# A four-layer decoder trunk: GpSimd makes the norm's diagonals and the recurrence's constants, and ScalarE's table functions keep program order

## The chip, the cores and the metric

One core of a Trainium2 chip runs the kernel in one launch. The metric is device time in microseconds (us), the median of several runs. In the profile, PE is TensorE's matmul, PEld its weight load, DVE is VectorE, ACT is ScalarE, POOL is GpSimd and SP is SyncE, whose queue issues the DMAs.

## The reference

The input is 256 tokens of width 1024 in float32. Four layers follow each other; each is a token mixer and a squared-ReLU MLP (1024 to 4096 to 1024), both behind an RMS norm and added to the residual. The mixers are a gated linear recurrence (layers 0 and 3), a chunked spatial gating unit (layer 1) and a short gated convolution (layer 2). A last RMS norm ends it. What matters here is the norm and the recurrence mixer:

```python
def _rmsnorm(x, g):
    x32 = x.astype(jnp.float32)
    y = x32 * lax.rsqrt(jnp.mean(x32 * x32, axis=-1, keepdims=True) + EPS)
    return y.astype(x.dtype) * g

def _rglru_mixer(h, w_in, conv_w, conv_b, gate_a_w, gate_a_b, gate_x_w, gate_x_b, lam, w_out):
    gate, xr = jnp.split(h @ w_in, 2, axis=-1)          # D_RNN = 1280 each
    gate = jax.nn.gelu(gate)
    xr = _causal_dwconv(xr, conv_w) + conv_b
    xh = xr.reshape(b, s, A_HEADS, A_HEAD_DIM)
    r = jax.nn.sigmoid(jnp.einsum("bshi,hij->bshj", xh, gate_a_w).reshape(b, s, D_RNN) + gate_a_b)
    ig = jax.nn.sigmoid(jnp.einsum("bshi,hij->bshj", xh, gate_x_w).reshape(b, s, D_RNN) + gate_x_b)
    log_a = -LRU_C * r.astype(jnp.float32) * jax.nn.softplus(-lam.astype(jnp.float32))
    a = jnp.exp(log_a)
    u = jnp.sqrt(-jnp.expm1(2.0 * log_a)) * (ig * xr).astype(jnp.float32)
    _, hs = lax.associative_scan(_lru_combine, (a, u), axis=1)   # h = a * h_before + u
    return (hs.astype(h.dtype) * gate) @ w_out

def _sqrelu_mlp(h, w1, w2):
    return jnp.square(jax.nn.relu(h @ w1)) @ w2
```

## The kernel before

**Layout.** Features lie on the 128 partitions and the 256 tokens along the free dimension. Eight feature tiles make up the residual. Intermediates are kept in pairs of two tiles (128 x 512).

**Products.** Each float32 product is made of three TensorE matmuls of a rounded format: the weight is split into a high and a low part, the activation too, and high by high, high by low and low by high are added up (`mm3`, L164). Weights come in chunks of up to 2048 columns by DMA from SP's queue into `raw`; ACT casts each 1024 columns to the high part (`whi`, L135), DVE subtracts to get the low part (`wlo`, L136). These two steps are called the cast and the split of the weights below. Up to five chunks are held at a time, so a new cast can begin when PE has finished with an old chunk. The gates' block-diagonal weights and the spatial weights are used whole, in plain float32 (L451, L578).

**The norm.** The gain is multiplied into the activations at once (`prep`, L195 and L196), and the token's scale 1/rms is applied after the product, when the result is read from PSUM. `Scales.first` sums the squares over the features with a small matmul (L245), then makes the reciprocal root without a table: ACT copies the sum (L228), and POOL does a seed and three Newton steps, 13 operations of 128x2 (L229 to L235), and splits the result into a high and a low part (L251, L252). Four multiplies of the 128x128 unit matrix by a column of these (L257, on DVE) make diagonal matrices `diag`. `Scales.second` multiplies them by ones on PE (L263), which lays the scales along the free dimension in every partition, and ACT copies that row to SBUF (L267, `rs`). `first` and `second` are called from hooks within the running product, in most places five of the eight steps of a 512-column product apart. The last norm of all uses the square root's table and DVE instead (`table=True`).

**The recurrence mixer** goes through `LRU_ORDER`: three branch products with the short convolution behind them (L417 to L436), a first gate product with GELU (`gated`, L489, L490), the two gates of the first five tiles (`gates(0)`, L451 and tanh at L455), the recurrence of pairs 0 and 1 (`recur`), the gates of the other five tiles, the recurrence of pairs 2 to 4, and the rest of the gate products. `recur` makes the decay by tanh and exp (L467) with per-channel constants `lam2` and `lam4`, takes a square root (L475), ends the coefficient with an affine step on DVE (L478) and runs the scan (L481). `meet` multiplies state and gate (L498) and splits the result (L329 on ACT, L330 on DVE) for the output product. `softplus_lambda` makes the constants at the start from a series in s = t / (t + 2), on DVE (L386 to L401, each 128x20).

**Order.** PE's instructions keep the order in which they are written. Those of the other engines are put in order ahead of time by a scheduler, by priority and by a model of when each is ready; every engine then runs its own queue strictly in that order. `recur` and the second half of `Scales.first` have raised priority, the weights' loads, casts and splits lowered.

Of the kernel before, what the change touches and what calls it, by code (L numbers as in the profile page):

```python
# [9 lines left out]
F32 = mybir.dt.float32  # L10
F32R = mybir.dt.float32r
I32 = mybir.dt.int32
AF = mybir.ActivationFunctionType
# [16 lines left out]
LRU_C = 8.0  # L30
# [41 lines left out]
def trunk(ctx: ExitStack, tc: tile.TileContext, xT, consts, sbias, weights, out, widths, whole, causal):  # L72
    nc = tc.nc
    MULT, ADD, SUB, MAX = ALU.mult, ALU.add, ALU.subtract, ALU.max
# [24 lines left out]
    def wtile(dtype=F32, name="wk"):  # L99
        return wide.tile([P, 2, T], dtype, name=name, tag="wk", bufs=N_WIDE)  # L100

    def bank():
        return psum.tile([P, 512], F32, name="ps", tag="ps")
# [39 lines left out]
    def next_chunk():  # L143
        i = used[0]
        used[0] += 1
        while asked[0] < n_chunks:
            ahead = sum(n not in whole for n in range(i + 1, asked[0]))
            if asked[0] > i and ahead + (asked[0] not in whole) > AHEAD:
                break
            with tc.high_priority(offset=-LATER):  # L150
                for load, part in fetch(asked[0]):
                    load()
                    part()
            asked[0] += 1
        return ready.pop(i)
# [17 lines left out]
    eye = const.tile([P, P], F32, name="eye")  # L173
# [64 lines left out]
    class Scales:  # L238
# [3 lines left out]
        def first(self, table=False):  # L242
            ps = bank()
            for c in range(2):
                nc.tensor.matmul(ps[:, 2 * c:2 * c + 2], sq_now[0][:, c * P:(c + 1) * P], ones[:, :2],  # L245
                                 start=True, stop=True)
            with tc.high_priority(offset=SOON):
                self.col = rsqrt(ps[:, 0:4].rearrange("p (c two) -> p c two", two=2)[:, :, 0], table)
                eng = nc.vector if table else nc.gpsimd
                hi, lo = (work.tile([P, 2], F32R, name="rc2", tag="rc2", bufs=4) for _ in range(2))  # L250
                eng.tensor_copy(out=hi, in_=self.col)  # L251
                eng.tensor_tensor(out=lo, in0=self.col, in1=hi.bitcast(F32), op=SUB)  # L252
                self.diag = []
                for part in (hi, lo):
                    diag = work.tile([P, 2, P], F32R, name="diag", tag="diag", bufs=4)
                    for c in range(2):
                        nc.vector.tensor_scalar_mul(diag[:, c, :], eye, part.bitcast(F32)[:, c:c + 1])  # L257
                    self.diag.append(diag.rearrange("p c t -> p (c t)"))

        def second(self, copy=True):  # L260
# [8 lines left out]
    def both(r):  # L269
        return r.unsqueeze(1).broadcast_to([P, 2, T])  # L270
# [102 lines left out]
    lam2 = const.tile([P, 2 * KR], F32, name="lam2")  # L373
    lam4 = const.tile([P, 2 * KR], F32, name="lam4")
    half_b = const.tile([P, 4 * KR], F32, name="half_b")

    def softplus_lambda():

        n = 2 * KR

        def small():
            return work.tile([P, n], F32, name="sp", tag="sp", bufs=8)

        lam = cst[:, CONST_AT["a_lam"]:CONST_AT["a_lam"] + n]
        neg, mag, t, d, s, s2, q = (small() for _ in range(7))
        nc.vector.tensor_scalar_mul(neg, lam, -1.0)  # L386
        nc.vector.tensor_tensor(out=mag, in0=lam, in1=neg, op=MAX)
        nc.scalar.activation(t, mag, AF.Exp, scale=-1.0)
        nc.vector.tensor_scalar_add(d, t, 2.0)
        nc.vector.reciprocal(out=d, in_=d)  # L390
        nc.vector.tensor_tensor(out=s, in0=t, in1=d, op=MULT)
        nc.vector.tensor_tensor(out=s2, in0=s, in1=s, op=MULT)
        nc.vector.tensor_scalar_mul(q, s2, 1.0 / 19.0)
        for i in range(17, 1, -2):
            nc.vector.scalar_tensor_tensor(out=q, in0=q, scalar=1.0 / i, in1=s2, op0=ADD, op1=MULT)
        nc.vector.scalar_tensor_tensor(out=q, in0=q, scalar=1.0, in1=s, op0=ADD, op1=MULT)
        nc.vector.tensor_scalar_max(neg, neg, 0.0)
        nc.vector.scalar_tensor_tensor(out=q, in0=q, scalar=2.0, in1=neg, op0=MULT, op1=ADD)
        nc.vector.tensor_scalar_mul(lam2, q, LRU_C / 4)
        nc.vector.tensor_scalar_mul(lam4, q, -LRU_C / 2)  # L400
        nc.vector.tensor_scalar_mul(half_b, cst[:, CONST_AT["a_ba"]:CONST_AT["a_ba"] + 4 * KR], 0.5)  # L401

    def mixer_a(layer):
        scale = Scales()
        xc = []
        beside = {}
        for g in range(KR // GRP):
            pairs = [wtile(name="be") for _ in range(2)]
            beside.update({(g, m + 1): pairs[m // 2][:, m % 2, :] for m in range(GRP - 2)})
        rg, ig = ([wtile(name=n) for _ in range(KR // 2)] for n in ("rg", "ig"))  # L410
# [28 lines left out]
        def gates(g):  # L439

            own = [xc[(g * GRP + m) // 2][:, (g * GRP + m) % 2, :] for m in range(GRP)]
            near = [own[1]] + [beside[g, m] for m in range(1, GRP - 1)] + [own[GRP - 2]]
            at = 0
            for m in range(GRP):
                mt = g * GRP + m
                ps = bank().rearrange("p (j t) -> p j t", t=T)
                for e in range(2):
                    for n, x in enumerate((own[m], near[m])):
                        if at % 8 == 0:
                            w = next_chunk().rearrange("p (k w) -> p k w", w=P)  # L450
                        nc.tensor.matmul(ps[:, e, :], w[:, at % 8, :], x, start=n == 0, stop=n == 1)  # L451
                        at += 1
                for e, dst in enumerate((rg, ig)):
                    c = (2 * e + layer) * KR + mt
                    nc.scalar.activation(dst[mt // 2][:, mt % 2, :], ps[:, e, :], AF.Tanh, scale=0.5,  # L455
                                         bias=half_b[:, c:c + 1])

        def recur(pairs):


            th, qs = {}, {}
            for i in pairs:
                th[i], qs[i] = wtile(name="th"), wtile(name="q")
                for dst, fn, lam in ((th[i], AF.Tanh, lam2), (qs[i], AF.Exp, lam4)):
                    for j in range(2):
                        c = layer * KR + 2 * i + j
                        nc.scalar.activation(dst[:, j, :], rg[i][:, j, :], fn, scale=lam[:, c:c + 1],  # L467
                                             bias=lam[:, c:c + 1])
                nc.vector.tensor_scalar_add(qs[i], qs[i], 1.0)
                t = rg[i]  # L470
                nc.vector.scalar_tensor_tensor(out=t, in0=th[i], scalar=1.0, in1=qs[i], op0=ADD, op1=MULT)
                nc.vector.scalar_tensor_tensor(out=qs[i], in0=t, scalar=4.0, in1=qs[i], op0=SUB, op1=MULT)
                nc.vector.scalar_tensor_tensor(out=ig[i], in0=ig[i], scalar=1.0, in1=xc[i], op0=ADD, op1=MULT)
            for i in pairs:
                nc.scalar.activation(th[i], th[i], AF.Sqrt)  # L475
                nc.vector.scalar_tensor_tensor(out=th[i], in0=qs[i], scalar=-0.25, in1=th[i], op0=MULT, op1=MULT)
                nc.vector.tensor_tensor(out=ig[i], in0=ig[i], in1=th[i], op=MULT)  # L477
                nc.vector.tensor_scalar(out=qs[i], in0=qs[i], scalar1=-0.5, scalar2=-1.0, op0=MULT, op1=ADD)  # L478
                h = xc[i]
                for j in range(2):  # L480
                    nc.vector.tensor_tensor_scan(out=h[:, j, :], data0=qs[i][:, j, :], data1=ig[i][:, j, :],  # L481
                                                 initial=0.0, op0=MULT, op1=ADD)
                hs.append(h)

        def gated(nm):

            for ps in in_mm(nm):
                gate = wtile(name="gate")
                nc.vector.tensor_tensor(out=gate, in0=ps, in1=both(scale.row), op=MULT)  # L489
                nc.scalar.activation(gate, gate, AF.Gelu_apprx_tanh)  # L490
                gs.append(gate)
                meet()

        def meet():

            while 2 * min(len(hs), len(gs)) > len(srcs):
                i = len(srcs) // 2
                nc.vector.tensor_tensor(out=hs[i], in0=hs[i], in1=gs[i], op=MULT)  # L498
                srcs.extend(tiles_of(split(hs[i])))
# [156 lines left out]
    for i in range(2):  # L656
        for load, part in fetch(i, step=512):
# [3 lines left out]
            steps.append(part)  # L661
    asked[0] = 2
    softplus_lambda()
    for k in range(KD):
        prep(k, "mix_g", 0)
# [11 lines left out]
    scale = Scales()  # L677
    scale.first(table=True)
    xg = []
    for i in range(KD // 2):  # L680
        t = wtile(name="xg")
# [131 lines left out]
```

## Time and profile before

| | us |
|---|---|
| median of 3 runs | 1093.14 (1092.78 to 1093.72) |
| the profiled execution's own time | 1093.35 |
| its span, first to last instruction | 1091.6 |
| PE busy | 1066.9 |
| DVE busy | 734.8 |
| ACT busy | 609.7 |
| POOL busy | 36.1 |

In the timeline's rows the columns are start, duration, engine, line, operation, output and inputs, shapes and count; in brackets stands the idle time of that engine ahead of it and what ended it. A row with a count above one joins neighbours, and its duration is from the start of the first to the end of the last. Matmuls overlap each other: one lasts 277 ns in the rows, though in an undisturbed stretch 9 begin per us, so PE's pace is read from counts. In the waits, the columns are the total, how often, and the longest. In the stretches, each engine's busy time is followed by its count of instructions, then come PE's granted clock as a share of the full one, the DMA engines' share and GB/s. In groups by line stand busy us and the mean in ns, and then the engine's idle time ahead.

### The profile page before, as it was taken

To read this page: it belongs to the slowest core of one execution; us is meant where nothing else is said; L and a number is where in the kernel's file an instruction comes from. 1 tells how busy PE (TensorE), PEld (TensorE's weight loads), DVE (VectorE), ACT (ScalarE), POOL (GpSimd) and SP (SyncE) were. 2 spreads that over 40 slices of the span, in tenths; PEclk is the share of its full clock that TensorE was granted. 3 is DMA by queue.
4 is the path that set the end of the run, shared out by engine and by line. 5 is a ranking of instruction groups with operands and counts; after the bars stand their busy time and mean duration, and the time that the engine had idled before them with its cause. 6 is when DMAs were issued, how large, how long until landed. Compare 5 with 4: busy or idle time off the path is not lost.

```text
span 1091.6 us, 21721 instructions
## 1 busy us (share of the span) xinstructions
PE 1066.9 (98%) x9078; PEld 1055.7 (97%) x9078; DVE 734.8 (67%) x991; ACT 609.7 (56%) x847; POOL 36.1 (3%) x139
## 2 busy tenths in 40 slices
PE   7998999999999999999999999999999999999996
PEld 7997999999999999999999999999999989999995
DVE  6989866555748766555777775556579698655553
ACT  6699655444655555444644555445457896544442
POOL 1000100000020100000010010000010001000000
PEclk9998999999999999999999999999999999999998
DMA  9754765555466565555466466555545447555301
GB/s 329 265 210 135 246 230 189 197 194 195 159 208 207 182 211 192 195 193 194 157 211 208 159 219 204 195 194 190 197 151 198 155 133 249 202 199 195 124 1 39
DMA packets 58802, 204.97 MB, mean 188 GB/s; under 512 B 6480, under 2 KB 8656, under 8 KB 58704
## 3 DMA queue, kind: packets, MB, share of 16 engines
q1 hardware_dynamic: 58288, 203.19, 55.0%
q8 instruction: 71, 1.16, 0.4%
q10 hardware_dynamic: 416, 0.39, 0.1%
q14 instruction: 27, 0.22, 0.1%
HBM read 202.51 MB, written 1.05 MB: 186 GB/s over the span
## 4 chain that ended last, share of the span: by engine, by line
PE 84%; DVE 7%; ACT 5%; DMA 2%; issue 1%; POOL 1%; SPq 0%; DVEq 0%; ACTq 0%; POOLq 0%
PE ps L164 80%; DMA raw<-weights 2%; PE ps L542 2%; DVE wlo L136 2%; DVE xc L481 1%; ACT q L467 1%; PE ps L451 1%; DVE xc L429 1%; ACT th L467 1%; ACT whi L135 1%; DVE ig L477 1%; ACT rg L455 0%; ACT L475 0%; ACT ig L455 0%; POOL rc L229 0%
## 5 line engine op out<-in xcount | busy, mean ns | idle before, releaser
L136 DVE TENSOR_TENSOR wlo<-raw,whi 128x1024 fp32r<-128x1024 f32 (+1 forms) x376 | 443.6, 1211 | 225.9 <-ACT whi L135 225.9
L135 ACT CAST whi<-raw 128x1024 fp32r<-128x1024 f32 (+1 forms) x376 | 376.1, 1038 | 325.2 <-issue 290.9
L164 PE MATMUL ps<-xs,whi 128*128 128x256 f32 x3200 | 550.7, 277 | 6.6 <-ACT whi L135 6.5
L164 PEld LDWEIGHTS ps<-xs,whi 128*128 128x128 f32 x3200 | 484.4, 188 | 7.0 <-ACT whi L135 6.5
L164 PE MATMUL ps<-xs,wlo 128*128 128x256 f32 x1600 | 442.9, 277 | 0.0
L164 PE MATMUL ps<-hi,whi 128*128 128x256 f32 x1312 | 363.7, 277 | 4.6 <-ACT hi L329 4.6
L164 PE MATMUL ps<-lo,whi 128*128 128x256 f32 x1312 | 364.1, 278 | 1.8 <-DVE lo L330 1.6
L164 PE MATMUL ps<-hi,wlo 128*128 128x256 f32 x1312 | 363.5, 277 | 0.7 <-DVE wlo L136 0.7
L164 PEld LDWEIGHTS ps<-xs,wlo 128*128 128x128 f32 x1600 | 301.3, 188 | 0.2 <-DVE wlo L136 0.2
L164 PEld LDWEIGHTS ps<-hi,whi 128*128 128x128 f32 x1312 | 247.6, 189 | 4.8 <-ACT hi L329 4.8
L164 PEld LDWEIGHTS ps<-lo,whi 128*128 128x128 f32 x1312 | 247.5, 189 | 2.9 <-DVE lo L330 2.5
L164 PEld LDWEIGHTS ps<-hi,wlo 128*128 128x128 f32 x1312 | 247.6, 189 | 0.9 <-DVE wlo L136 0.9
L344 DVE SCALAR_TENSOR_TENSOR u<-ps,rs 128x512 f32<-128x512 f32 x64 | 44.0, 687 | 33.2 <-PE ps L164 33.2
L346 ACT ACTIVATE hi<-u 128x512 fp32r<-128x512 f32 x64 | 40.3, 630 | 35.1 <-DVE u L344 35.1
L348 DVE TENSOR_TENSOR lo<-hsq,hi 128x512 fp32r<-128x512 f32 x64 | 44.1, 689 | 14.8 <-ACT hsq L347 12.2
L195 ACT ACTIVATE xs<-x,cst 128x256 fp32r<-128x256 f32 x64 | 29.4, 501 | 30.2 <-DVE x L315 29.1
L347 ACT ACTIVATE hsq<-u 128x512 f32<-128x512 f32 x64 | 39.4, 615 | 0.0
L196 DVE SCALAR_TENSOR_TENSOR xs<-x,cst,xs 128x256 fp32r<-128x256 f32 x64 | 28.8, 482 | 8.7 <-ACT xs L195 8.7
L229 POOL TENSOR_SCALAR rc<-rc 128x2 int32<-128x2 int32 x9 | 9.9, 1096 | 723.4 <-ACT rc L228 723.4
L257 DVE TENSOR_SCALAR diag<-eye,rc 128x128 fp32r<-128x128 f32 x36 | 8.1, 286 | 30.9 <-POOL rc L251 30.9
L451 PE MATMUL ps<-xc,raw 128*128 128x256 f32 x112 | 28.4, 379 | 0.0
L429 DVE SCALAR_TENSOR_TENSOR xc<-xr,cst,xc 128x255 f32<-128x255 f32 (+2 forms) x60 | 25.4, 481 | 0.8 <-ACT xc L425 0.6
(111 smaller groups left out, 476.0 us busy)
## 6 DMA issues: line engine op xcount, KB each, us to landing
raw<-weights SPq DMA_DIRECT2D x377, 512.0 KB, 4.7
raw<-weights SPq DMA_DIRECT2D x12, 256.0 KB, 4.5
x<-xT SPq DMA_DIRECT2D x8, 128.0 KB, 4.3
sb<-sbias SPq DMA_DIRECT2D x2, 256.0 KB, 4.9
outT<-o SPq DMA_DIRECT2D x2, 256.0 KB, 2.3
outT<-o ACTq DMA_DIRECT2D x1, 256.0 KB, 2.3
cst<-consts SPq DMA_DIRECT2D x1, 132.0 KB, 2.2
outT<-o ACTq DMA_DIRECT2D x1, 128.0 KB, 1.8
```

The source lines that it names most:

```text
L135: nc.scalar.copy(out=hi[:, s], in_=raw[:, e])
L136: nc.vector.tensor_tensor(out=lo[:, s], in0=raw[:, e], in1=hi.bitcast(F32)[:, s], op=SUB)
L164: nc.tensor.matmul(ps, a, b, start=start and n == 0, stop=stop and n == 2, skip_group_check=True)
L195: nc.scalar.activation(xs[:, hi], x, AF.Copy, scale=g)
L196: nc.vector.scalar_tensor_tensor(out=xs[:, lo], in0=x, scalar=g, in1=xs.bitcast(F32)[:, hi], op0=MULT, op1=SUB)
L344: nc.vector.scalar_tensor_tensor(out=u, in0=ps, scalar=0.0, in1=both(scale.row), op0=MAX, op1=MULT)
L346: nc.scalar.activation(hi, u, AF.Square)
L347: nc.scalar.activation(sq, u, AF.Square)
L348: nc.vector.tensor_tensor(out=lo, in0=sq, in1=hi.bitcast(F32), op=SUB)
L429: nc.vector.scalar_tensor_tensor(out=conv[:, j, d:], in0=raw[:, j, :T - d], scalar=tap(i), in1=conv[:, j, d:], op0=MULT, op1=ADD)
L451: nc.tensor.matmul(ps[:, e, :], w[:, at % 8, :], x, start=n == 0, stop=n == 1)
L467: nc.scalar.activation(dst[:, j, :], rg[i][:, j, :], fn, scale=lam[:, c:c + 1], bias=lam[:, c:c + 1])
```

## The change

Four edits.

1. In `Scales.first`, the four multiplies that make the diagonals run on the engine that also made the split ahead of them: POOL, except in the last norm, where it stays DVE.
2. In `softplus_lambda`, everything behind the reciprocal runs on POOL. There a fused multiply-add becomes two instructions, so 15 DVE instructions become 25 on POOL. The maximum with zero stays on DVE and comes ahead.
3. In `recur`, the affine step on `qs` (L478 before) moves from DVE to ACT, and the square roots of all pairs of a call come ahead of the pairs' further steps.
4. Tanh, exp, square root and GELU of the recurrence mixer are called through `function`, which ties each of them to the one before, so that the scheduler leaves them in the order in which they are written. This adds no semaphore: they are all in ACT's queue.

```diff
@@ Scales.first
-                        nc.vector.tensor_scalar_mul(diag[:, c, :], eye, part.bitcast(F32)[:, c:c + 1])
+                        eng.tensor_scalar_mul(diag[:, c, :], eye, part.bitcast(F32)[:, c:c + 1])
@@ softplus_lambda
+        def add_mult(out, a, c, b, op0=ADD, op1=MULT):
+            nc.gpsimd.tensor_scalar(out=out, in0=a, scalar1=c, scalar2=None, op0=op0)
+            nc.gpsimd.tensor_tensor(out=out, in0=out, in1=b, op=op1)
...
-        nc.vector.tensor_tensor(out=s, in0=t, in1=d, op=MULT)
-        nc.vector.tensor_tensor(out=s2, in0=s, in1=s, op=MULT)
-        nc.vector.tensor_scalar_mul(q, s2, 1.0 / 19.0)
+        nc.vector.tensor_scalar_max(neg, neg, 0.0)
+        nc.gpsimd.tensor_tensor(out=s, in0=t, in1=d, op=MULT)
+        nc.gpsimd.tensor_tensor(out=s2, in0=s, in1=s, op=MULT)
+        nc.gpsimd.tensor_scalar_mul(q, s2, 1.0 / 19.0)
         for i in range(17, 1, -2):
-            nc.vector.scalar_tensor_tensor(out=q, in0=q, scalar=1.0 / i, in1=s2, op0=ADD, op1=MULT)
-        nc.vector.scalar_tensor_tensor(out=q, in0=q, scalar=1.0, in1=s, op0=ADD, op1=MULT)
-        nc.vector.tensor_scalar_max(neg, neg, 0.0)
-        nc.vector.scalar_tensor_tensor(out=q, in0=q, scalar=2.0, in1=neg, op0=MULT, op1=ADD)
-        nc.vector.tensor_scalar_mul(lam2, q, LRU_C / 4)
-        nc.vector.tensor_scalar_mul(lam4, q, -LRU_C / 2)
+            add_mult(q, q, 1.0 / i, s2)
+        add_mult(q, q, 1.0, s)
+        add_mult(q, q, 2.0, neg, MULT, ADD)
+        nc.gpsimd.tensor_scalar_mul(lam2, q, LRU_C / 4)
+        nc.gpsimd.tensor_scalar_mul(lam4, q, -LRU_C / 2)
...
+    last_fn = []
+
+    def function(*args, **kw):
+        ins = nc.scalar.activation(*args, **kw).ins
+        if last_fn:
+            tc.add_manual_dep(ins, last_fn.pop().name,
+                              mybir.DependencyInfo(mybir.DependencyClass.NoSync, mybir.DependencyReason.DATA),
+                              reason="tables")
+        last_fn.append(ins)
@@ gates, recur, gated: the table functions
-                    nc.scalar.activation(dst[mt // 2][:, mt % 2, :], ps[:, e, :], AF.Tanh, ...)
+                    function(dst[mt // 2][:, mt % 2, :], ps[:, e, :], AF.Tanh, ...)
...
-                        nc.scalar.activation(dst[:, j, :], rg[i][:, j, :], fn, ...)
+                        function(dst[:, j, :], rg[i][:, j, :], fn, ...)
...
-                nc.scalar.activation(gate, gate, AF.Gelu_apprx_tanh)
+                function(gate, gate, AF.Gelu_apprx_tanh)
@@ recur
             for i in pairs:
-                nc.scalar.activation(th[i], th[i], AF.Sqrt)
+                function(th[i], th[i], AF.Sqrt)
+            for i in pairs:
                 nc.vector.scalar_tensor_tensor(out=th[i], in0=qs[i], scalar=-0.25, in1=th[i], op0=MULT, op1=MULT)
                 nc.vector.tensor_tensor(out=ig[i], in0=ig[i], in1=th[i], op=MULT)
-                nc.vector.tensor_scalar(out=qs[i], in0=qs[i], scalar1=-0.5, scalar2=-1.0, op0=MULT, op1=ADD)
+                nc.scalar.activation(qs[i], qs[i], AF.Copy, scale=-0.5, bias=-1.0)
```

More of the change, by code (lines that the diff above doesn't have):

```diff
@@ L454, in gates @@
                     c = (2 * e + layer) * KR + mt
-                    nc.scalar.activation(dst[mt // 2][:, mt % 2, :], ps[:, e, :], AF.Tanh, scale=0.5,
-                                         bias=half_b[:, c:c + 1])
+                    function(dst[mt // 2][:, mt % 2, :], ps[:, e, :], AF.Tanh, scale=0.5, bias=half_b[:, c:c + 1])
         def recur(pairs):
@@ L466, in recur @@
                         c = layer * KR + 2 * i + j
-                        nc.scalar.activation(dst[:, j, :], rg[i][:, j, :], fn, scale=lam[:, c:c + 1],
-                                             bias=lam[:, c:c + 1])
+                        function(dst[:, j, :], rg[i][:, j, :], fn, scale=lam[:, c:c + 1], bias=lam[:, c:c + 1])
                 nc.vector.tensor_scalar_add(qs[i], qs[i], 1.0)
```

## The prediction

> **What bounds the kernel now.** I read the busy times first, then stretches of PE's matmul count, then who waited for whom, then the timeline around PE's few holes.
>
> ```profile
> span 1091.6 us, 21721 instructions
> PE 1066.9 (98%) x9078; PEld 1055.7 (97%) x9078; DVE 734.8 (67%) x991; ACT 609.7 (56%) x847; POOL 36.1 (3%) x139
> ```
>
> PE is the bound: time is won only where PE has a hole, and a new hole is lost time. The next rows (PE alone, busy time and matmul count by stretch) show the two large holes, each beside an undisturbed stretch just ahead of it.
>
> ```profile
> 76.00:92.00 16.00, 16.00 (x144) 1.00 0.53 165
> 92.00:108.00 16.00, 11.17 (x68) 0.79 0.28 85
> 868.00:884.00 16.00, 16.00 (x142) 1.00 0.05 18
> 884.00:892.00 8.00, 5.73 (x47) 1.00 0.41 126
> ```
>
> At 144 per 16 us the first hole (end of the recurrence mixer, layer 0) lacks 76 matmuls, 8.4 us; some 0.21 x 16 = 3.4 us of that is the lower granted clock (0.79), the rest waiting. The second (the same place in layer 3) lacks 71 - 47 = 24 matmuls, 2.7 us. So 11.1 us is all that better recurrence work can win. The waits name the causes:
>
> ```profile
> PE ps L164 <- ACT hi L329: 4.6, 1, 4.6
> PE ps L263 <- DVE diag L257: 2.6, 2, 2.2
> DVE diag L257 <- POOL rc L251: 30.9, 8, 4.1
> ```
>
> The third line matters most for this change. Eight times DVE stands still for about 3.9 us, in its queue's order, because its next instruction is a diagonal and POOL is still computing the reciprocal root. That costs PE little (second line). Whoever takes the diagonals off DVE lets DVE run in exactly these eight windows.
>
> **The diagonals (L257) move to POOL.** Four multiplies of 128x128 follow POOL's chain of 15 small operations. A typical window, and the first and last rows of the three that look like it (372, 547, 635):
>
> ```profile
> 635.48 0.19 POOL L229 TENSOR_SCALAR rc<-rc 128x2 int32<-128x2 int32 x1 [83.74 <-ACT rc L228]
> 639.33 0.20 POOL L252 TENSOR_TENSOR rc<-rc,rc 128x2 fp32r<-128x2 f32 x1
> 636.66 2.00 ACT L135 CAST whi<-raw 128x1024 fp32r<-128x1024 f32 x2 [1.27 <-DMA raw<-weights]
> 640.11 2.35 DVE L136 TENSOR_TENSOR wlo<-raw,whi 128x1024 fp32r<-128x1024 f32 x2
> 641.98 0.40 PE L263 MATMUL ps<-diag,ones_r 128*128 128x256 f32 x2
> 372.85 0.19 POOL L229 TENSOR_SCALAR rc<-rc 128x2 int32<-128x2 int32 x1 [48.81 <-ACT rc L228]
> 379.35 0.40 PE L263 MATMUL ps<-diag,ones_r 128*128 128x256 f32 x2
> ```
>
> POOL needs 639.53 - 635.48 = 4.05 us, a pitch of 0.28. PE comes to the diagonals 6.50 us after POOL's start and needs the second half 0.12 later. The price of a diagonal on POOL is not shown; the nearest row is POOL's only 128x128 operation:
>
> ```profile
> 1.14 0.29 POOL L174 TENSOR_SCALAR_AFFINE_SELECT eye<-ones 128x128 f32<-128x128 f32 x1 [0.63 <-DVE ones L170]
> ```
>
> With the 0.08 us between POOL's operations that is 0.37 each, 1.5 us for four (from below, at the chain's pitch of 0.28, 1.1). Alone, POOL is done 5.55 us after its start, inside the 6.62. But the two weight splits (L136) that DVE runs after the diagonals have their input from 637.7 and 638.7 on (the two casts at 636.66), so they will now run inside POOL's chain. What a split does to POOL stands here:
>
> ```profile
> 123.94 5.76 DVE L136 TENSOR_TENSOR wlo<-raw,whi 128x1024 fp32r<-128x1024 f32 x5
> 127.58 2.18 POOL L229 TENSOR_SCALAR rc<-rc 128x2 int32<-128x2 int32 x1 [101.44 <-ACT rc L228]
> 128.76 2.01 ACT L135 CAST whi<-raw 128x1024 fp32r<-128x1024 f32 x2 [1.27 <-PE ps L164]
> 133.41 0.20 POOL L252 TENSOR_TENSOR rc<-rc,rc 128x2 fp32r<-128x2 f32 x1
> 134.07 0.64 PE L263 MATMUL ps<-diag,ones_r 128*128 128x256 f32 x2
> ```
>
> The same POOL operation that takes 0.19 took 2.18 and ended at 129.76, 0.06 after DVE's run of splits (129.70). POOL stands while DVE splits. It can also be the other way round: this select ended at 285.07, and the second split beside it was stretched to make 3.25 us of a usual 2.35:
>
> ```profile
> 282.90 3.25 DVE L136 TENSOR_TENSOR wlo<-raw,whi 128x1024 fp32r<-128x1024 f32 x2 [3.08 <-ACT whi L135]
> 283.50 1.57 POOL L643 TENSOR_SCALAR_AFFINE_SELECT raw<-raw 128x1024 f32<-128x1024 f32 x1 [149.90 <-DMA raw<-weights]
> ```
>
> So the two take turns, and a POOL operation may slip in between two splits, but the chain of 19 is put off by about the two splits, 2.35 us, whichever comes first. The window then ends 4.05 + 1.5 + 2.35 = 7.9 us after its start, against 6.62: PE waits 1.3 us, three times, 3.9 us. The other windows:
>
> ```profile
> 810.31 0.19 POOL L229 TENSOR_SCALAR rc<-rc 128x2 int32<-128x2 int32 x1 [170.78 <-ACT rc L228]
> 816.13 0.40 PE L263 MATMUL ps<-diag,ones_r 128*128 128x256 f32 x2
> 914.89 2.00 ACT L135 CAST whi<-raw 128x1024 fp32r<-128x1024 f32 x2 [1.21 <-PE ps L164]
> 920.15 0.20 POOL L252 TENSOR_TENSOR rc<-rc,rc 128x2 fp32r<-128x2 f32 x1
> 920.76 0.69 PE L263 MATMUL ps<-diag,ones_r 128*128 128x256 f32 x2 [0.40 <-DVE diag L257]
> 307.24 0.20 POOL L252 TENSOR_TENSOR rc<-rc,rc 128x2 fp32r<-128x2 f32 x1
> 308.21 0.40 PE L263 MATMUL ps<-diag,ones_r 128*128 128x256 f32 x2
> 25.94 0.20 POOL L252 TENSOR_TENSOR rc<-rc,rc 128x2 fp32r<-128x2 f32 x1
> 26.72 4.62 DVE L136 TENSOR_TENSOR wlo<-raw,whi 128x1024 fp32r<-128x1024 f32 x4
> 27.26 0.40 PE L263 MATMUL ps<-diag,ones_r 128*128 128x256 f32 x2
> ```
>
> - Layer 3's mixer: PE comes after 5.82 (+0.12); 7.9 - 5.94 = 1.95 us.
> - Layer 0's MLP: POOL ends at 133.61 + 1.5 + 2.35 = 137.45; PE's second matmul now runs at about 134.35; 3.1 us.
> - Layer 3's MLP: 920.35 + 3.85 = 924.2 against about 921.15; 3.1 us.
> - Layer 1's mixer: ACT has no cast in that window, so only the diagonals count: 307.44 + 1.5 = 308.95 against 308.33; 0.6 us.
> - Layer 0's mixer: four splits wait behind the diagonals; 26.14 + 1.5 + 4.6 = 32.2 against 27.38; PE stands 4.9 us. This PE delay lies ahead of the 8.4 us hole, where PE waits for DVE and ACT anyway. Those two have done the four splits early and lose about 1.5 us (the row of scales comes 4.9 later, but DVE only reached its first use at 31.3). I charge the 1.5 below.
>
> Sum of the windows: 3.9 + 1.95 + 3.1 + 3.1 + 0.6 = 12.6 us lost. Bounds: 2.0 without any split in the way (135.1 against 134.35, 921.85 against 921.15, and the 0.6), and about 20 if the third split of each run gets in too (1.2 us in six windows). I take 12.6, since the casts stand in the rows.
>
> **The recurrence's constants move to POOL.** Some 25 operations of 128x20 at 0.28 are 7.0 us, in turns with DVE's start-up work from about 5 us on. The recurrence is the first to use the result, behind all branch products, so they cost nothing unless POOL still works at them when the first root arrives at 21.1: see the third rival. DVE's relief there (about 1.5 us) buys nothing, since PE does not wait there.
>
> **The table functions in program order, and the affine step on ACT.** Table loads and the steps concerned, by line, in layer 0's mixer (the two DVE/ACT steps' means from there and from the whole run):
>
> ```profile
> L490 ACT ACT_TABLE_LOAD x3 | 3.8, 1283 | 0.1
> L475 ACT ACT_TABLE_LOAD x3 | 3.8, 1283 | 0.1
> L455 ACT ACT_TABLE_LOAD x2 | 2.6, 1283 | 0.0
> L467 ACT ACT_TABLE_LOAD x1 | 1.3, 1283 | 0.0
> L475 ACT ACTIVATE th<-th 128x512 f32<-128x512 f32 x5 | 2.9, 626 | 0.0
> L478 DVE TENSOR_SCALAR q<-q 128x512 f32<-128x512 f32 x10 | 4.2, 416 | 0.0
> ```
>
> Nine loads; program order needs six (GELU, exp, root, exp, root, GELU), so three fall away, 3.85 us of ACT, all at the end of the mixer where the hole is. ACT gains five affine steps of about 0.63, 3.1 us, DVE loses five of 0.42, 2.1 us; each scan now waits for a step on ACT, which may stand behind a 1.0 us cast. The trade is small for ACT (-0.7) and better for DVE. What the order itself does: a gate's tanh no longer comes after roots of the pairs behind it (one of the two loads at L455), and the GELU of the third pair no longer before a root (L490 and L475 lose one each). Per layer I bound the gain by 0 and by the hole (8.4 and 2.7). In layer 0 I estimate 3.0 (2.1 of DVE, which paces this stretch, and part of a load), less the 1.5 charged above: 1.5. In layer 3 the delay is in the windows already; I take 2.5, since two of the three loads (2.6) nearly cover 2.7.
>
> [...]
>
> **Sum.** +12.6 - 1.5 - 2.5 = +8.6 us on the profiled execution's own 1093.35: 1101.95. The median of the runs is 0.21 lower (1093.14), so I forecast 1101.7.
>
> **The rivals.**
> - *Faster: the splits stay out of POOL's windows*, because DVE's queue holds something else there, or POOL slips through. Then the windows cost 2.0, the start costs nothing, layer 0 wins 3.5 and layer 3 2.5: 1093.35 + 2.0 - 6.0 = 1089.3, and 1084 if both holes close. For it: the select that got in between two splits. Against: 2.18 for 0.19, and the casts at 636.66. It decides from there on where the two splits put POOL off by less than about a third of 2.35.
> - *No change: the holes close whole* (11.1) against 12.6: 1094.9.
> - *Slower still: start-up.* POOL still computes the constants when the first root comes; all 7.0 us behind it would make the PE delay 11.9, 3.5 more than the hole hides, and a wait of that length halves the clock as the 4.6 us wait did: +3 on the sum each, near 1108. [...]
> - *The order changes nothing*: as many loads as before, or scans stand for ACT's step as long as the loads saved. Then the gains go: 1093.35 + 12.6 + 1.5 = 1107.4.
>
> **How the numbers follow.** Chances: forecast 0.52, splits kept out 0.22, holes closed 0.10, start-up 0.10, order without effect 0.06. A change under 0.2% (2.2 us) cannot be told from none here. Slower is the forecast's 0.52, start-up, order (0.68 less a little for a forecast that lands near zero): 0.66; same 0.09, mostly the closed holes; faster 0.25, the kept-out splits and part of the closed holes. The forecast's own range, with 1 to 3 us of delay per window, is 1096 to 1106; with the others 1087 to 1108, which leaves out the best end of the first rival and little above.
>
> **What would show it.** Right: DVE no longer waits for POOL (30.9 gone), splits stand inside POOL's windows, single POOL operations there last 1 us or more, and PE waits for POOL's diagonals some 1 to 3 us in six windows. The third: the last constants on POOL after 21 us. The order: six loads in 56 to 110, and more than 68 matmuls in the hole. The forecast is wrong if PE's waits for the diagonals sum to less than about 5 us.

## The result, and the profile after

The changed kernel takes 1117.22 us (median, 1116.06 to 1118.30) against 1093.41 for the kernel before (1092.78 to 1093.72): a ratio of 1.0217, 95% interval 1.0205 to 1.0230, so 23.8 us slower. The forecast was 1101.7 with a range of 1087 to 1108: the direction was right, and where most of the loss stands; the size was not. The profiled execution of the changed kernel took 1116.06 us, its span is 22.5 us longer.

The page of the kernel after:

```profile
span 1114.1 us, 21742 instructions
...
PE 1073.0 (96%) x9078; PEld 1058.6 (95%) x9078; DVE 725.9 (65%) x934; ACT 607.8 (55%) x851; POOL 76.2 (7%) x196
```

PE has the same 9078 matmuls and 22.5 us more time in which to do them. DVE lost 57 instructions, POOL gained 57. The waits of the kernel after (total, times, longest):

```profile
PE ps L263 <- POOL diag L257: 16.8, 16, 4.6
PE ps L164 <- DVE lo L330: 5.1, 4, 2.5
...
PE ps L164 <- ACT hi L329: 0.4, 1, 0.4
```

PE now waits 16.8 us for the diagonals, where it waited 0.4 for DVE's diagonals outside the last norm. DVE's 30.9 us of standing for POOL is gone from the list. The old hole's wait for `hi` (4.6) is nearly gone too, and stands one line further, at `lo`. PE's matmuls on the diagonals, from the timeline of the kernel after; the number in brackets is PE's wait:

```profile
32.38 0.58 PE L263 MATMUL ps<-diag,ones_r 128*128 128x256 f32 x1 [4.64 <-POOL diag L257]
33.53 0.58 PE L263 MATMUL ps<-diag,ones_r 128*128 128x256 f32 x1 [0.57 <-POOL diag L257]
139.37 0.39 PE L263 MATMUL ps<-diag,ones_r 128*128 128x256 f32 x1 [1.15 <-POOL diag L257]
141.61 0.39 PE L263 MATMUL ps<-diag,ones_r 128*128 128x256 f32 x1 [1.85 <-POOL diag L257]
...
388.53 0.38 PE L263 MATMUL ps<-diag,ones_r 128*128 128x256 f32 x1 [0.34 <-POOL diag L257]
389.69 0.39 PE L263 MATMUL ps<-diag,ones_r 128*128 128x256 f32 x1 [0.78 <-POOL diag L257]
...
830.92 0.39 PE L263 MATMUL ps<-diag,ones_r 128*128 128x256 f32 x1 [1.01 <-POOL diag L257]
832.08 0.39 PE L263 MATMUL ps<-diag,ones_r 128*128 128x256 f32 x1 [0.77 <-POOL diag L257]
...
939.72 0.38 PE L263 MATMUL ps<-diag,ones_r 128*128 128x256 f32 x1 [0.60 <-POOL diag L257]
941.91 0.42 PE L263 MATMUL ps<-diag,ones_r 128*128 128x256 f32 x1 [1.81 <-POOL diag L257]
```

Every window of POOL's chain has become a stall of PE, two waits each, because the second half of the diagonals comes after the first. Why, is seen in a typical window, the one that the prediction worked out (POOL's rows, then DVE's, of the kernel after):

```profile
381.53 0.19 POOL L229 TENSOR_SCALAR rc<-rc 128x2 int32<-128x2 int32 x1 [48.85 <-ACT rc L228]
...
384.01 1.07 POOL L232 TENSOR_TENSOR rc<-rc 128x2 f32<-128x2 f32 x1
385.16 1.06 POOL L233 TENSOR_TENSOR rc<-rc 128x2 f32<-128x2 f32 x1
...
387.28 2.35 POOL L257 TENSOR_SCALAR diag<-eye,rc 128x128 fp32r<-128x128 f32 x4
383.80 2.36 DVE L136 TENSOR_TENSOR wlo<-raw,whi 128x1024 fp32r<-128x1024 f32 x2 [2.53 <-ACT whi L135]
```

DVE runs two splits from 383.80 to 386.16, and beside them two of POOL's operations of 0.2 us take 1.07 and 1.06. POOL is done at 389.63, 8.10 us after its start; the prediction said 7.9. Two parts of that stand differently: the splits cost 1.7 us instead of 2.35, and four diagonals take 2.35 us (0.59 each) instead of 1.5.

The start is the worst window. POOL and DVE there, kernel after:

```profile
15.68 0.52 POOL L404 TENSOR_SCALAR lam<-sp 128x20 f32<-128x20 f32 x1
22.22 1.17 POOL L229 TENSOR_SCALAR rc<-rc 128x2 int32<-128x2 int32 x1 [6.01 <-ACT rc L228]
...
27.21 1.23 POOL L235 TENSOR_TENSOR rc<-rc 128x2 f32<-128x2 f32 x1
...
19.61 8.78 DVE L136 TENSOR_TENSOR wlo<-raw,whi 128x1024 fp32r<-128x1024 f32 x7 [0.65 <-ACT whi L135]
```

The constants are done at 16.2 us, 6.0 us ahead of the first root: they are in nobody's way. Then DVE splits seven times in a row, and five operations of POOL's chain take 1.14 to 1.23 us each.

The stretches that answer to the two holes shown of before, with PE alone (length, busy time and count, granted clock), and the start:

```profile
26.00:42.00 16.00, 10.79 (x74) 0.79 0.93 360
80.00:96.00 16.00, 16.00 (x143) 1.00 0.38 132
96.00:112.00 16.00, 12.50 (x105) 1.00 0.40 135
881.00:897.00 16.00, 16.00 (x143) 1.00 0.11 34
897.00:905.00 8.00, 6.61 (x58) 1.00 0.21 68
```

The hole at the end of layer 0's mixer now lacks 38 matmuls instead of 76, and layer 3's 13 instead of 24. A new hole stands at the start: in 26 to 42 us 74 matmuls ran, at 144 per 16 us 70 too few.

Stage lengths, from the start of one of PE's sums of squares (L245) to the next, say where the 22.5 us lie. They are worked out from the start times of those nine rows in each trace (differences before rounding):

| us | layer 0 mixer | mlp 0 | mixer 1 | mlp 1 | mixer 2 | mlp 2 | layer 3 mixer | mlp 3 |
|---|---|---|---|---|---|---|---|---|
| before | 106.8 | 174.1 | 71.2 | 174.8 | 87.8 | 174.8 | 103.4 | 168.8 |
| after | 110.8 | 177.2 | 72.8 | 176.5 | 89.4 | 176.5 | 108.5 | 172.3 |
| difference | +4.0 | +3.1 | +1.6 | +1.6 | +1.6 | +1.7 | +5.1 | +3.4 |

### The profile page after: what moved, and what is told of

It reads as the page before. It is cut to its first block, busy times and chain, and to the rows that moved or that the text cites. A ratio compares the mean times of both kernels' runs of the same rounds, so it can differ in the third digit from the quotient of the medians.

```text
span 1114.1 us, 21742 instructions
## 1 busy us (share of the span) xinstructions
PE 1073.0 (96%) x9078; PEld 1058.6 (95%) x9078; DVE 725.9 (65%) x934; ACT 607.8 (55%) x851; POOL 76.2 (7%) x196
## 4 chain that ended last, share of the span: by engine, by line
PE 77%; POOL 4%; DVE 3%; ACT 2%; issue 1%; DMA 0%; POOLq 0%; DVEq 0%; ACTq 0%
PE ps L164 74%; POOL diag L257 2%; PE ps L556 1%; PE ps L466 1%; POOL rc L232 1%; POOL rc L233 1%; DVE wlo L136 0%; ACT th L411 0%; POOL rc L235 0%; DVE xc L495 0%; DMA raw<-weights 0%; ACT q L411 0%; ACT L411 0%; PE ps L263 0%; POOL rc L234 0%
## 5 line engine op out<-in xcount | busy, mean ns | idle before, releaser
L229 POOL TENSOR_SCALAR rc<-rc 128x2 int32<-128x2 int32 x9 | 6.2, 690 | 699.5 <-ACT rc L228 699.5
L263 PE MATMUL ps<-diag,ones_r 128*128 128x256 f32 x18 | 7.5, 426 | 19.3 <-POOL diag L257 16.8
```

## The experiments

**Which edit costs?** Each edit was made alone; what was left out of one is the rest of the change.

*diag_only*: before plus edit 1.

```diff
-                        nc.vector.tensor_scalar_mul(diag[:, c, :], eye, ...)
+                        eng.tensor_scalar_mul(diag[:, c, :], eye, ...)
```

> The kernel before with the first edit alone: the diagonals on POOL. Theory A (POOL's windows: DVE's splits hold POOL up, POOL's diagonals are slow, and the clock falls behind the longer waits): this edit carries nearly all of the loss, 1112 to 1118 us, and PE's waits for the diagonals are 16 to 20 us. Theory B (the two recurrence mixers, which lost 4.0 and 5.1 us of the 22.5, lost them through the new order and the affine step on ACT): this edit costs only the other five windows, about 13 us, so 1105 to 1108.

Measured: 1120.49 us, ratio 1.0249 (1.0235 to 1.0263). One line carries the whole loss and 3 us more. That is theory A's cause, 2.5 us above its range; PE waits 20.2 us for the diagonals. The profiled span is 6.7 us longer than the changed kernel's. Most of that goes with the granted clock: between the start and the last norm it is at half for seven stretches of 3.41 us, in the changed kernel for four (0.985 and 0.990 in the mean), and each costs up to 1.7 us, half of its length.

*consts_only*: before plus edit 2.

> The kernel before with the second edit alone: the recurrence's constants on POOL. Both theories: within 1 us of the kernel before, 1092 to 1094.5, since POOL has finished with them (16.2 us after the start in the changed kernel) before the first sum of squares is there. A start that is late by the 1.1 us that the first 512-column cast came later (17.3 for 16.1) would show as up to +1.

Measured: 1093.66, ratio 1.0001 (0.9992 to 1.0010). The constants cost and give nothing, as both theories had it.

*recur_only*: before plus edits 3 and 4.

> The kernel before with the third and fourth edit alone: table functions in program order, roots batched, affine step on ACT. Theory A: the two holes at the ends of the recurrence mixers shrink or stay, 1086 to 1094 us. Theory B: the mixers get longer, 1098 to 1103 us.

Measured: 1094.63, ratio 1.0012 (1.0003 to 1.0020). No gain, and no great loss: between the two theories. The six table loads that were forecast are there (group of table loads, 56 to 112 us, kernel after):

```profile
L411 ACT ACT_TABLE_LOAD x6 | 7.7, 1283 | 0.1
```

What took their place, in the kernel with both recurrence edits (ACT, DVE, then PE at the hole; its L406 holds all the table functions, L490 is the scan), and last the kernel before's roots of pairs 2 and 3, `hi` and `lo`:

```profile
90.51 1.68 ACT L406 ACTIVATE th<-th 128x512 f32<-128x512 f32 x3
97.37 0.62 ACT L329 CAST hi<-xc 128x512 fp32r<-128x512 f32 x1
97.86 1.22 DVE L136 TENSOR_TENSOR wlo<-raw,whi 128x1024 fp32r<-128x1024 f32 x1
99.00 1.26 DVE L490 TENSOR_TENSOR_SCAN xc<-q,ig 128x256 f32<-128x256 f32 x2
100.18 0.66 DVE L330 TENSOR_TENSOR lo<-xc,hi 128x512 fp32r<-128x512 f32 x1
98.04 0.58 PE L164 MATMUL ps<-hi,whi 128*128 128x256 f32 x1 [5.32 <-ACT hi L329]
100.90 0.58 PE L164 MATMUL ps<-lo,whi 128*128 128x256 f32 x1 [2.27 <-DVE lo L330]
...
87.56 1.15 ACT L475 ACTIVATE th<-th 128x512 f32<-128x512 f32 x2
96.50 0.62 ACT L329 CAST hi<-xc 128x512 fp32r<-128x512 f32 x1 [0.73 <-DVE xc L498]
97.15 0.69 DVE L330 TENSOR_TENSOR lo<-xc,hi 128x512 fp32r<-128x512 f32 x1
```

The three roots run together, so pair 2, the first that PE needs, waits until tanh and exp of all three pairs are done: its root runs at 90.51 instead of 87.56. Its `hi` comes 0.87 us later than before (97.37 against 96.50) and its `lo` 3 us later (100.18 against 97.15). PE waits 7.6 us there instead of 4.6. The larger part of `lo`'s delay stands in DVE's queue, which takes a split of the weights and two scans ahead of it. Whether the batching also caused that order is not shown.

*order_only* (edit 4 and the order of edit 3, affine step on DVE) and *affine_only* (only the affine step) split this once more.

> The kernel before with the table functions in program order and the three roots together, but the affine step left on DVE; the diagonals and the constants stay on DVE. Both edits together gave 1094.6 us against 1093.6 (ratio 1.0012). Theory A: the batching itself holds pair 2 back, because its root now stands behind the tanh and exp of pairs 3 and 4 and of the last gate; then this edit alone gives no gain either, 1092.5 to 1096, and PE's wait at the end of layer 0's mixer stays between 4.5 and 7.6 us in total. Theory B: the order would have paid for three table loads a layer (3.85 us) and the affine step on ACT took it back, by a scan that waits for ACT; then this edit alone gives 1086 to 1091.

Measured: 1094.34, ratio 1.0007 (0.9998 to 1.0016); PE waits 5.4 and 1.7 us in the hole. Theory A: the order alone already gains nothing.

> The kernel before with only the affine step moved to ACT. Theory A (of the two edits the batching is the one that costs): the trade of 0.63 us on ACT for 0.42 us on DVE is nearly neutral, 1091.5 to 1095. Theory B (the affine step is the one that costs): a scan waits for ACT behind a cast of 1.0 us or a table load of 1.28 us, once or twice in the critical part of layers 0 and 3: 1095 to 1099.

Measured: 1094.39, ratio 1.0009 (1.0000 to 1.0018). Neutral, as theory A has it: layer 0's mixer is 1.2 us longer than before, layer 3's 0.9 shorter.

**Why does the diagonal cost so much?** *hold_dve*: the changed kernel with one DVE instruction more, a copy of one element of the last diagonal, so that DVE's queue stands until POOL is done, as in the kernel before, and no split from behind that copy can run in POOL's chain.

```diff
+                if not table:
+                    hold = work.tile([P, 1], F32, name="hold", tag="hold", bufs=2)
+                    nc.vector.tensor_copy(out=hold, in_=diag.bitcast(F32)[:, 1, :1])
```

> The changed kernel, and after the last diagonal of each norm (not the last norm) one DVE copy of 128x1 that reads it, so that DVE's queue stands until POOL is done, as it stood before; the copy's result is not used. Theory A, contention: POOL's chain runs undisturbed, each of its operations 0.2 us, the chain ends 6.4 us after its start (4.05, and 2.35 for the diagonals), PE waits about 5 to 6 us in all instead of 16.8, no clock fall: 1095 to 1103 us. If it is only POOL's own slowness and not the contention, the time stays at 1112 to 1118. Theory B: the mixers' loss stays, 1104 to 1109.

Measured: 1101.53, ratio 1.0074 (1.0061 to 1.0088), theory A. An instruction that only makes DVE idle wins 15.7 us. In the norms' eight windows 19 of POOL's 128x2 operations last over 1 us in the changed kernel, 4 here and 4 in the kernel before; PE waits 4.3 us for POOL. Its window, POOL's last row and DVE's held copy:

```profile
383.19 2.35 POOL L257 TENSOR_SCALAR diag<-eye,rc 128x128 fp32r<-128x128 f32 x4
385.58 0.15 DVE L261 COPY hold<-diag 128x1 f32<-128x1 f32 x1 [6.65 <-POOL diag L257]
```

*late_row* and *mid_row* leave the splits where they are and let PE ask later: its matmuls on the diagonals stand three or four steps of the matmul loop later in late_row (one in layer 3's mixer), two in mid_row (there not in the mixers of layers 0 and 3).

```diff
-            nxt_banks = in_mm(4, {3: scale.second} if b == 1 else {})
+            nxt_banks = in_mm(4, {5: scale.second} if b == 1 else {})   # late_row: 7
```

> The changed kernel with nothing but a later place for PE's two matmuls that read the diagonals: 3 or 4 steps of the matmul loop later in the MLPs, in layers 0, 1 and 2's mixers (a step of 12 matmuls is 1.36 us), one step of 0.7 us in layer 3's mixer. POOL's chain and the splits beside it stay as they are. Theory A: the loss is only that PE asks before POOL is done (waits of 16.8 us in all, and the half clock behind them): the waits fall to 1 to 3 us, and 1117.2 becomes 1095 to 1102. Theory B: POOL's turns with DVE cost elsewhere too (splits that are stretched, weights that come late, work on DVE that bunches up behind the later row): waits of PE turn up at other lines and it stays above 1105.

Measured: 1129.55, ratio 1.0331 (1.0317 to 1.0345), slower still. The waits say why:

```profile
PE ps L164 <- ACT hi L346: 13.4, 4, 3.3
...
PE ps L263 <- POOL diag L257: 5.1, 4, 3.4
```

The wait for POOL fell to 5.1 us as hoped, but the row of scales then came too late for the first hidden tile of each of the four MLPs, 3.3 us each: my two theories had both missed that the row has a reader with a deadline of its own. Twelve stretches of 3.41 us ran at half clock, against four in the changed kernel (0.978 and 0.990 in the mean). At this size of delay, theory B's outcome.

> The changed kernel with PE's diagonal matmuls two steps of the matmul loop later in the MLPs and the mixers of layers 1 and 2 (2.7 us, 1.4 us in layer 1), the mixers of layers 0 and 3 as they are in the changed kernel. late_row moved them by four steps: the wait for POOL went from 16.8 to 5.1 us, but the first hidden tile of an MLP then came 3.3 us late, four times (13.4 us), and layer 0's mixer lost more. Theory A (PE's wait is only a matter of the deadline, which has some room behind it): the waits in mlp 1, mlp 2, the mixers of layers 1 and 2 go (1.6 us each), those of mlp 0 and mlp 3 (3.0 and 2.4) fall to about 0.5, and the hidden tiles cost 0 to 0.6 each; 11 us less, up to 3.4 more where a fall of the clock goes too: 1102 to 1107. Theory B (the row has no room behind it at all: what PE doesn't wait for the diagonal, it waits for the hidden tile): 1112 to 1118.

Measured: 1104.90, ratio 1.0103 (1.0089 to 1.0116), 12.3 us better than the changed kernel, as theory A has it. One of the two places that were left alone, and a typical window:

```profile
31.34 0.58 PE L263 MATMUL ps<-diag,ones_r 128*128 128x256 f32 x1 [4.46 <-POOL diag L257]
...
387.02 0.40 PE L263 MATMUL ps<-diag,ones_r 128*128 128x256 f32 x2
```

Where PE asks later the wait for POOL is gone, but for 1.6 us in mlp 0, and mixers 1 and 2 are back at 71.2 and 87.8 us. So POOL's turns with DVE cost nothing in themselves there; they cost through PE's deadline.

**What is the rest?** *diag_hold* (before, edit 1 and the held DVE) and *no_diag* (the change without edit 1).

> The kernel before with the diagonals on POOL and DVE held by a copy of one element of the last diagonal (it stands as it does in the kernel before; the copy's result is not used), recurrence and constants as before. Theory A (hold_dve's extra 4.2 and 1.8 us are the recurrence's): layer 0 at 107 to 108.5, layer 3's mixer at 103 to 104, in all 1095 to 1098, of which 2 to 4 are POOL's slower diagonals in six windows. Theory B (they are POOL's late first chain and the late diagonals): layer 0 at 110 to 111.5, in all 1098 to 1102.

Measured: 1101.94, ratio 1.0084 (1.0067 to 1.0101). Stages: layer 0's mixer 108.9, mlp 0 176.0, mixer 1 72.8, layer 3's mixer 103.9, mlp 3 170.7. Neither theory: layer 0 lies between both, the time in theory B's range, layer 3's mixer in theory A's.

> The changed kernel with the diagonals back on DVE: constants on POOL, affine step on ACT, table order. From PE's first scale matmul to that of layer 0's MLP the kernel before takes 106.8 us, recur_only 109.7, hold_dve 111.0; in layer 3's mixer 103.4, 104.6 and 105.2. Theory A (the recurrence's edits carry these terms and the constants on POOL nothing): 109 to 110 and 104 to 105 us, in all 1093.5 to 1096. Theory B (the +4.2 of hold_dve is POOL's late first chain): layer 0 at 107 to 108, in all 1092 to 1094.

Measured: 1095.42, ratio 1.0013 (1.0003 to 1.0022). Layer 0's mixer 109.3, layer 3's 104.6; all others as before or up to 1.1 shorter. Theory A. With diag_hold this adds up: in layer 0, +2.5 from the recurrence and +2.1 from POOL's late diagonals make 4.6, and with both (hold_dve) it is +4.2; in layer 3, +1.2 and +0.5 against +1.8. Without the held DVE it doesn't add up: layer 0's mixer is 5.5 us longer in diag_only, 2.5 in no_diag, and only 4.0 with both.

**Can the hole be closed by order?** Three kernels tried.

*pair_first*: order_only, but pair 2 goes through its recurrence alone.

```diff
-    ("recur", (2, 3, 4)), ("gated", 2), ("gated", 4),
+    ("recur", (2,)), ("gated", 2), ("recur", (3, 4)), ("gated", 4),
```

> The order edit as in order_only (affine step on DVE), but the recurrence of the last three pairs is cut in two: pair 2 goes through its roots and its gate's GELU alone, then pairs 3 and 4; two more table switches a layer than with the three together. PE's order of matmuls is unchanged. Theory A: PE's hole is set by when pair 2 comes out, and the batching (or, in the kernel before, the interleaving) holds it for the other pairs. Worked out from rows of the kernel with both recurrence edits: pair 2's tanh and exp end at 85.1, root load 86.4, root 87.1, then 0.7 + 0.7 + 1.3 of scans + 0.7 product, hi and lo by about 92 us, where PE arrives at 92.5; the 4.6 us wait and the half clock behind it go, and a wait of 2 to 3 us for pair 3 comes at about 98. Layer 0 gains 3 to 6 us, layer 3 0 to 2: 1086 to 1091. Theory B: the hole is set by ACT's total of work, loads among it: with two loads more (2.6 us) it is no smaller, 1093 to 1098.

Measured: 1101.86, ratio 1.0076 (1.0063 to 1.0090). Pair 2's `hi` came at 92.21 us, as worked out, though weight casts stood between; pair 3's then came at 106.29 and PE waited 6.3 us for it. No gain, as in theory B, and 4 us slower than its range.

*prio_only*, *order_prio*, *recur_prio*: a higher priority for the four steps behind a scan, on top of before, order_only and recur_only.

```diff
+                with tc.high_priority(offset=300):
                     gate = wtile(name="gate")
                     ...
                     meet()
```

> The kernel before, with a higher priority for the gate's product, its GELU, the final product and its split into hi and lo (the four steps behind a scan), so that DVE and ACT take them ahead of the recurrence of the pairs behind. Theory A (what sets PE's 4.6 us hole in layer 0 is where DVE's queue puts pair 2's last steps: scans done at 93.1, product only at 95.8): pair 2's hi and lo come 1.5 to 2.5 us earlier and the hole shrinks by as much, but each GELU now stands between roots and costs a load of 1.28 us more, which pair 3 pays: 1089 to 1094. Theory B (the hole is conserved: DVE's 23 us of work for the three pairs and ACT's loads set when the last pair is out, and PE waits there what it doesn't wait for pair 2): 1093 to 1098.

> The same priority on top of order_only (table functions in program order, three loads fewer a layer, affine step on DVE). Theory A: order_only lost its saved loads (3.85 us) because DVE and ACT used the time for steps of pairs 3 and 4 and for weights (lo of pair 2 stood behind them); with the last steps first, pair 2's lo is ready by about 96 us instead of 97.8 to 100.8 and the others follow in time: PE's waits at the end of layer 0's mixer fall from 7 to about 3 us and with them part of the half clock, 1086 to 1091. Theory B (conserved hole): 1093 to 1097.

> The same priority on top of recur_only, which has the affine step on ACT too. Theory A: as order_prio, and DVE, which is full from 84 to 100 us, has 0.42 us less per pair while ACT has room for 0.63 us: 1085 to 1090. If the affine step on ACT costs by itself (a scan that waits behind a weight cast), it is 1 to 3 us above order_prio. Theory B: 1093 to 1097.

Measured: 1100.00 (ratio 1.0057, 1.0044 to 1.0071), 1094.24 (1.0005, 0.9996 to 1.0014) and 1095.25 (1.0014, 1.0005 to 1.0023). Theory B twice, and prio_only worse than both theories. PE's waits at the hole of prio_only:

```profile
99.79 0.39 PE L164 MATMUL ps<-hi,whi 128*128 128x256 f32 x1 [1.63 <-ACT whi L135]
102.70 0.58 PE L164 MATMUL ps<-hi,wlo 128*128 128x256 f32 x1 [2.41 <-DVE wlo L136]
```

PE no longer waits for any activation there: it waits 4.0 us for the weights' casts and splits, which were pushed back. Layer 0's mixer is 0.7 us shorter than before, but mlp 0 is 2.9 and layer 3's mixer 1.4 longer. In the kernels with DVE's diagonals the wait at this place changes its name (pair 2's `hi`, its `lo`, pair 3, a weight), and its sum stays between 4.0 and 10.3 us. That fits what the kernel before shows there (length, then busy time and count of PE, PEld, DVE, ACT, POOL, then clock and DMA):

```profile
84.00:92.00 8.00, 8.00 (x73) 8.00 (x72) 7.87 (x15) 7.92 (x14) 0.00 (x0) 1.00 0.54 169
92.00:100.00 8.00, 3.25 (x16) 2.76 (x16) 7.92 (x16) 7.17 (x9) 0.00 (x0) 0.80 0.00 0
```

DVE is full and ACT nearly, so a step that is taken ahead puts another one off. That no order at all could close the hole is not shown; none of those tried did, and no version that ran beats the kernel before.

## Why the prediction was right or wrong

**The main mechanism: right, and shown.** Splits stand in POOL's windows, single operations there last over 1 us, and PE waits in all the windows named (16.8 us; the prediction's own line for being wrong was below 5). By medians, the loss of 23.7 us against these runs' before (1093.5) splits into three: splits in POOL's chain, with the half clock behind the longer waits, 15.7 (changed kernel less hold_dve); the diagonals on POOL without them, DVE's longer standing included, 6.1 (hold_dve less no_diag); and everything else 1.9 (no_diag less before).

**The windows: the term was too small.** The prediction gave 12.6 us for seven stages; they took 18.2 (before rounding), of which 1.2 belong to layer 3's recurrence (no_diag), so 17.0. Two steps failed.
- The price of a diagonal on POOL: 0.37 us was taken from the select, 0.59 is measured. Against that the two splits cost 1.7 in the row above, not 2.35, so the three alike windows came out at 1.6 to 1.7 instead of 1.3. In mixer 1, where no new split runs beside the chain, most of the miss (1.6 for 0.6) is the diagonals' 2.35 for 1.5.
- The clock: the sum of the windows holds PE's waits alone, up to 3.1 us, and no fall of the clock behind any of them. It fell behind 1.8 us in layer 3's mixer (0.50 from 832.90 us on) and behind 2.4 in mlp 3 (0.50 from 942.13 on), 3.41 us at half speed each time, which is 1.7 us of work each, 3.4 in all. The kernel before had already shown such a fall: the prediction names one, behind the 4.6 us wait (0.50 from 96.72 to 103.55 us), but there is another in the last norm, behind a window in which PE still worked for 0.58 us (the kernel before, PE alone; the last section has more):

```profile
1079.76:1083.17 3.41, 0.58 (x4) 1.00 0.01 2
1083.17:1086.58 3.41, 0.88 (x2) 0.50 0.00 0
```

**The recurrence: wrong.** The prediction counted three loads of 1.283 us less per layer, which came true, and with DVE's relief booked 3.0 and 2.5 us of gain. None came: 1094.6 for both edits alone. The step that failed is the one from "ACT and DVE have less to do" to "the hole shrinks": with both edits PE's first pair is ready later, `hi` by 0.87 us and `lo` by 3. The rival that the order changes nothing, given 0.06, came true in its outcome for this part, but not for its reasons: the loads did fall to six, and the affine step on ACT alone was neutral. The sign that was to show the gain, more than 68 matmuls in the hole, came too (105), but by luck: PE reached the hole late, while in no_diag, which has the same recurrence, its waits there rose to 7.6 us. Layer 0's mixer got 2.5 us longer in no_diag, not 3.0 shorter; layer 3's 1.2 longer, not 2.5 shorter.

**The start: right in kind, too cheap.** PE stood 5.2 us (said: 4.9), and the clock fell behind it (0.50 from 30.77 to 37.60 us), which the forecast had not charged: 70 matmuls are missing in 26 to 42 us, 7.8 us at 9 per us. The step that failed is that the hole at the mixer's end hides all but 1.5 us of this: it lacks 38 matmuls fewer than before, so it took up about half. With POOL's held-up chain and the old recurrence (diag_only) the mixer is 5.5 us longer, where 1.5 was charged; in the changed kernel it is 4.0, and how these divide between the start and the recurrence is open.

**The sum.** Windows 4.4 us more, layer 0's mixer 5.5 (+4.0 where -1.5 was forecast), layer 3's recurrence 3.7: 13.6, and with the 8.6 forecast 22.2 of the 22.5 us of span.

The constants at nothing, six table loads, and DVE's 30.9 us of standing that goes away at no profit: all as said.

## What to carry to other kernels

An engine that stands idle in a profile may be what keeps another one quick: before work is taken off it, look at what its queue runs next, and whether the chain that somebody waits for gets slower beside that (POOL's operations of 0.19 us took 1.04 to 1.28 beside splits here). A fixed-order chain should be costed from its start to the moment when its reader asks, and the reader's reader has a deadline too: two loop steps later in six windows won 12.3 us, one to four later in all eight lost 12.3. Saving instructions by batching was worth nothing here, where the consumer takes the batch's items one by one and needs the first one early.

## What the runs showed of the hardware

**TensorE's granted clock went by fixed windows of 3.41 us, and about half a window idle was enough to halve it.** The granted clock in all traces changes only at whole multiples of 3.41 us from one another: after its first rise the changes follow each other by 25, 2 and 287 such windows in the kernel before, by 6, 2, 233, 1, 31, 1 and 47 in the changed one. Cut along that grid, with PE alone, the kernel after shows (window, length, busy time and count, granted clock):

```profile
136.57:139.99 3.42, 2.03 (x16) 1.00 1.00 393
139.99:143.40 3.41, 1.79 (x15) 1.00 0.67 233
143.40:146.81 3.41, 3.41 (x33) 1.00 0.36 109
829.49:832.90 3.41, 1.63 (x12) 1.00 0.81 282
832.90:836.32 3.42, 3.42 (x19) 0.50 0.05 20
938.72:942.13 3.41, 1.00 (x6) 1.00 0.48 185
942.13:945.54 3.41, 3.41 (x17) 0.50 0.47 154
```

In mlp 0 PE waits 3.0 us in all, but the grid cuts it into 1.39 and 1.62: no fall. In layer 3's mixer it waits only 1.78 us, all in one window: the next window runs at 0.50. I added up PE's idle time in every window at full clock. In the kernel before and the changed one that is 629 windows: the six with 1.78 us or more were each followed by half clock, the others, with 1.62 or less, never. In 16 traces (these two and the fourteen experiments), some 5000 windows, it was so for the 49 with 1.66 us or more, and never for the others, with 1.63 or less: 1.66 of 3.41 us, about 49%, was enough. Where the grid lies against the kernel's start differs from run to run (the clock first rises at 11.39 us in the kernel before, at 10.29 in the changed one, between 9.4 and 12.6 in all 16), so whether a wait like the 3.0 us in mlp 0 costs clock is partly luck.

**POOL's multiply of 128x128 by a column takes 0.59 us** (2.35 for four), twice its select of the same size (0.29); DVE takes 0.23 (a window of the kernel before):

```profile
376.66 0.91 DVE L257 TENSOR_SCALAR diag<-eye,rc 128x128 fp32r<-128x128 f32 x4 [4.06 <-POOL rc L251]
```

**One split stopped POOL for most of its length.** Beside splits of 1.22 us, POOL's operations of 128x2 took 1.04 to 1.28 us instead of 0.19, mostly one operation for each split; a few stood through several (1.93 us in mixer 1; 2.18 in mlp 0 and 2.71 in mlp 3 of the kernel before). In the kernel before and the changed one all 25 that took over 1 us ended 0.05 to 0.06 us after a split, and none that ran without a split beside it took more than 0.20. A chain of small operations lost about 0.9 to 1.1 us for each split that ran beside it.
